# Gates of the recurrence and scores of the windowed attention as pairs of 64-row products on the two halves of the array's rows

## The chip, the core and the metric

One core of a Trainium2 chip runs the kernel in one launch. The time is the device time in microseconds of that launch; most executions of a kernel agree within 0.3%. The engines, as the profile names them: PE is TensorE's matmul, PEld its weight load, DVE is VectorE, ACT is ScalarE, POOL is GpSimd, SP issues transfers.

## What is computed

One layer of a hybrid decoder over 1024 prompt tokens and 8 sample tokens (width 1024). A combined projection feeds three branches: a convolution with a gated linear recurrence, windowed attention (window 128, 16 query heads of 64 on 4 key heads), and cross-attention into 256 memory rows. The branches are merged by gates, projected, normalised, and go through a SwiGLU block. Two places matter here.

```python
def rg_lru(xc, h0, wa, ba, wx, bx, lam):          # LRU_BLOCKS = 16, LRU_BLOCK = 64
    xblk = xf.reshape(B, T, LRU_BLOCKS, LRU_BLOCK)
    r = jax.nn.sigmoid(jnp.einsum('btni,nij->btnj', xblk, wa).reshape(B, T, C) + ba)
    i = jax.nn.sigmoid(jnp.einsum('btni,nij->btnj', xblk, wx).reshape(B, T, C) + bx)
    ...
def swa_prompt(q, k, v, sinks):                   # HEAD_DIM = 64, WINDOW = 128, blocks of 128 tokens
    s = jnp.einsum('bnqkgd,bnmkd->bnkgqm', qb, kband) * scale
    ...
    p = sink_softmax(s, mask, sinks)
```

Both contract over 64 values: a gate block has 64 inputs, a head has 64 dimensions.

## The kernel before

Everything is computed transposed: channels lie on the 128 partitions, tokens along the free dimension. Products keep almost the precision of float32 by splitting each operand into a high part `h` (float32r) and the low remainder `l`, and adding three products, h·h, h·l and l·h (`mm3`, lines 111 to 118; lines 241 to 243 are the same three in the projection). ACT writes the high part (line 77), DVE the low one (line 78).

The stages in order of time: keys and values of the memory; the projection (`project`), 30 units of seven products, each product in two halves of twelve matmuls; between its steps `pump` advances the recurrences (`lru`), one for each of the 8 slices of 128 channels, and the sample tokens' cross-attention; then the prompt's cross-attention and the windowed attention (`windows`), into which products of the branch projections (`fill`, tiles `bra` and `brc`) are laid; then the rest of the branch projections, the output projection, the SwiGLU block and the last product with its normalisation. A scheduler puts each engine's instructions into one fixed order when the kernel is built; that order is static on the chip.

**Gates** (lines 750 to 758). For each slice `m` and each third of the 1032 tokens (344 columns), the two gates are made one after the other, with a step of the projection between them. The stationary weights are 128 by 128 blocks that hold two 64 by 64 blocks on the diagonal and zeros elsewhere: `wr` is 128 by 256, one half for each gate. Each gate is three matmuls over all 128 rows into a bank of the pool tag "o" (one bank), and one tanh by ACT over 128 partitions (line 757).

**Scores** (lines 581 to 591). For each key head `kv` and block `b` of 128 queries, four heads share the keys. A head's query tile has its high part on rows 0 to 63 and its low part on rows 64 to 127; the keys' high part stands twice in `ks[0]`, their low part twice in `ks[1]`. So two matmuls over 128 rows make all four partial products: eight matmuls a block, each with 256 columns (128 in the first block of a head, b = 0, which has no predecessor). Heads 0 and 1 go to one bank of the tag "s", heads 2 and 3 to the other; two banks carry that tag, and they serve the projection's tiles `uc` as well. DVE adds the mask and takes the minimum (line 590), ACT makes the exponentials (line 594), and the transposed weights (`bt`, line 611) go into the products with the values (`bo`, lines 616 and 617).

Of the kernel before, what the change touches and what calls it, by code (L numbers as in the profile page):

```python
# [10 lines left out]
F32 = mybir.dt.float32  # L11
F32R = mybir.dt.float32r
AF = mybir.ActivationFunctionType
ALU = mybir.AluOpType
# [4 lines left out]
P = 128  # L19
D = 1024  # L20
KT = D // P
TP = 1024
# [6 lines left out]
NF = 22  # L29
# [23 lines left out]
GELU_C = math.sqrt(2.0 / math.pi)  # L53
GELU_A = math.sqrt(0.044715)

V_BG, V_CW, V_CB, V_BA, V_BX, V_LAM = 0, 24, 56, 64, 72, 80
V_G1, V_B1, V_G2, V_B2, V_SNK, V_SNKD, V_EPS, V_N = 88, 96, 104, 112, 120, 136, 137, 138


class Builder:  # L60
# [489 lines left out]
    def win_load(self, kv):  # L550

        nc, ph = self.nc, self.ph
        rows = lambda i: slice((i % 2) * 64, (i % 2) * 64 + 64)
        q = []
        ks = [ph.tile([P, TP], F32R, tag="ks", name=f"ks{kv}_{e}", bufs=4) for e in range(2)]
        for e in range(2):
            for half in range(2):
                nc.sync.dma_start(ks[e][half * 64:(half + 1) * 64].bitcast(F32), self.scr["k"][rows(kv), kv // 2, e, :])
        for g in range(4):
            st = ph.tile([P, TP], F32R, tag="st", name=f"st{kv}_{g}", bufs=6)  # L560
            for e in range(2):
                nc.sync.dma_start(st[e * 64:(e + 1) * 64].bitcast(F32), self.scr["q"][rows(g), 2 * kv + g // 2, e, :])
            q.append(st)
        vs = ph.tile([P, 8, P], F32R, tag="vs", name=f"vs{kv}", bufs=2)
        nc.sync.dma_start(vs.bitcast(F32), self.scr["v"][:, :, kv * P:(kv + 1) * P])
        return ks, q, vs

    def win_scores(self, kv, ops, b):

        nc = self.nc  # L570
        nk = 2 if b else 1
        n = nk * P
        k0 = max(b - 1, 0) * P
        msk = self.mask[:, 256 - n:]
        ks, q, _ = ops
        snk = self.nsnk[:, 4 * kv:4 * kv + 4]
        st = self.sm.tile([P, 12], F32, tag="bst", name=f"bst{kv}_{b}", bufs=4)
        p = self.ph.tile([P, 4, 257], F32, tag="p", name=f"bp{kv}_{b}", bufs=3)
        pg = [p[:, g, :n] for g in range(4)]
        nc.gpsimd.tensor_copy(p[:, :, n], snk)  # L580
        for pr in range(2):
            s = self.bank("s", f"bs{kv}_{b}_{pr}")
            for u in range(2):
                qq = q[2 * pr + u][:, b * P:(b + 1) * P]
                o = s[:, u * 256:u * 256 + n]
                nc.tensor.matmul(o, qq, ks[0][:, k0:k0 + n], start=True, stop=False)
                nc.tensor.matmul(o, qq, ks[1][:, k0:k0 + n], start=False, stop=True)
            for u in range(2):
                g = 2 * pr + u
                nc.vector.tensor_tensor_reduce(pg[g], s[:, u * 256:u * 256 + n], msk, 1.0, snk[:, g:g + 1],  # L590
                                               ALU.add, ALU.min, st[:, g:g + 1])
        for g in range(4):
            x = p[:, g, :n + 1]
            nc.scalar.activation(x, x, AF.Exp, bias=st[:, g:g + 1], scale=-1.0, accum_out=st[:, 4 + g:5 + g])  # L594
        nc.vector.reciprocal(st[:, 8:12], st[:, 4:8])
        for g in range(4):
            r = st[:, 8 + g:9 + g]
            if g % 2:
                nc.scalar.mul(pg[g], pg[g], r)
            else:  # L600
                (nc.gpsimd if g else nc.vector).tensor_scalar_mul(pg[g], pg[g], r)
        return pg
# [75 lines left out]
    def lru_consts(self):  # L678

        nc = self.nc  # L680
        lam = self.vec[:, V_LAM:V_LAM + KT]
        w = self.cst.tile([P, 8 * KT], F32, name="lruc")
        self.sp2 = w[:, 0:8]
        self.hba, self.hbx = w[:, 8:16], w[:, 16:24]
        e, z, z2, acc, t = (w[:, 24 + 8 * i:32 + 8 * i] for i in range(5))
        self.nsnk = self.cst.tile([P, 16], F32, name="nsnk")
        nc.vector.tensor_scalar_mul(self.nsnk, self.vec[:, V_SNK:V_SNK + 16], -1.0)
        self.hbg = self.cst.tile([P, 24], F32, name="hbg")
        nc.vector.tensor_scalar_mul(self.hbg, self.vec[:, V_BG:V_BG + 24], 0.5)
        nc.vector.tensor_scalar_mul(self.hba, self.vec[:, V_BA:V_BA + 8], 0.5)  # L690
        nc.vector.tensor_scalar_mul(self.hbx, self.vec[:, V_BX:V_BX + 8], 0.5)
        nc.vector.scalar_tensor_tensor(t, lam, -1.0, lam, op0=ALU.mult, op1=ALU.max)
        nc.scalar.activation(e, t, AF.Exp, scale=-1.0)
        nc.vector.tensor_scalar_add(z, e, 2.0)
        nc.vector.reciprocal(z, z)
        nc.vector.tensor_mul(z, z, e)
        nc.vector.tensor_mul(z2, z, z)
        nc.vector.memset(acc, 1.0 / 17.0)
        for d in (15, 13, 11, 9, 7, 5, 3, 1):
            nc.vector.tensor_mul(acc, acc, z2)  # L700
            nc.vector.tensor_scalar_add(acc, acc, 1.0 / d)
        nc.vector.tensor_mul(acc, acc, z)
        nc.vector.tensor_scalar(t, lam, -1.0, 0.0, op0=ALU.mult, op1=ALU.max)
        nc.vector.scalar_tensor_tensor(t, acc, 2.0, t, op0=ALU.mult, op1=ALU.add)
        nc.vector.tensor_scalar_mul(self.sp2, t, 2.0)
        self.sp4n = self.cst.tile([P, KT], F32, name="sp4n")
        nc.vector.tensor_scalar_mul(self.sp4n, t, -4.0)
# [20 lines left out]
    def lru(self, m, xr, yr):  # L728

        nc, io, vec = self.nc, self.io, self.vec  # L730
        col = lambda base: vec[:, base + m:base + m + 1]
        stt = nc.vector.scalar_tensor_tensor
        wr = self.lr.tile([P, 256], F32, tag="wlr", name=f"wlr{m}", bufs=1)
        nc.sync.dma_start(wr, io["wlru"][m])
        cw = [col(V_CW + 8 * i) for i in range(4)]
        xc = self.zt(f"xc{m}")
# [7 lines left out]
        nc.gpsimd.tensor_copy(self.pconv[:, m, :], xr[:, TP - 3:TP])  # L744
        nc.gpsimd.tensor_copy(self.scvo[:, m, 0:2, :], buf[:, 1:3, :])
        nc.gpsimd.tensor_copy(self.scvo[:, m, 2, :], xr[:, TP:T])
        wgh, wgl = (self.lr.tile([P, 256], F32R, tag=f"wg{e}", name=f"wg{e}{m}", bufs=1) for e in "hl")
        self.split(wgh, wgl, wr)
        a, ti = self.zt(f"tr{m}"), self.zt(f"ti{m}")
        for c, (t0, n) in enumerate(THIRDS):  # L750
            xch, xcl = (self.lr.tile([P, n], F32R, tag=f"xc{e}", name=f"xc{e}{m}_{c}", bufs=1) for e in "hl")
            self.split(xch, xcl, xc[:, t0:t0 + n])
            yield
            for j, (dst, hb) in enumerate(((a, self.hba), (ti, self.hbx))):
                ps = self.bank("o", f"g{m}_{j}_{c}")[:, :n]
                self.mm3(ps, [((wgh[:, j * P:(j + 1) * P], wgl[:, j * P:(j + 1) * P]), (xch, xcl))])
                nc.scalar.activation(dst[:, t0:t0 + n], ps, AF.Tanh, bias=hb[:, m:m + 1], scale=0.5)
                yield

        sp2, sp4n = self.sp2[:, m:m + 1], self.sp4n[:, m:m + 1]  # L760
# [21 lines left out]
        g = self.zt(f"ge{m}")  # L782
# [563 lines left out]
class Finish:  # L1346
# [42 lines left out]

_INS = {  # L1390
    "xT": (P, KT, T), "xQ": (2, 4, P, 4 * QN), "memT": (P, KT * NM), "wmk": (KT, P, D), "wmv": (8, P, D), "win": (60, P, D),
    "wbr": (24, P, D), "wout": (KT, P, D), "wgu": (2 * NF, P, D), "wdn": (KT, P, NF * P), "wlru": (KT, P, 256),
    "vec": (P, V_N), "cst": (P, P + 256), "scv": (P, KT, 3, NB), "sh": (P, KT, NB), "cwk": (NB, P, 256),
    "cwv": (NB, P, 256), "cwkT": (NB, P, 2, P), "cmk": (NB, NM, D), "cmvT": (NB, D, NM),
}
# [7 lines left out]
def _pack(i):  # L1403
    import numpy as np

    f = {k: np.asarray(v) for k, v in i.items()}

    def mtiles(w):
        k, m = w.shape
        return w.reshape(k // P, P, m // P, P).transpose(2, 1, 0, 3).reshape(m // P, P, k)  # L1410
# [4 lines left out]
    def cols(v):  # L1415
        return v.reshape(-1, P).T

    o = {}
    x = np.concatenate([f["x_prompt"].reshape(TP, D), f["x_sample"].reshape(NB, D)], axis=0)
# [9 lines left out]
    o["wout"] = mtiles(f["w_out"][0])  # L1429
    o["wgu"] = mtiles(f["w_gate_up"][0])  # L1430
    o["wdn"] = mtiles(f["w_down"][0])
    blk = np.zeros((KT, P, 256), np.float32)
    for j, name in enumerate(("lru_wa", "lru_wx")):
        w = f[name][0].reshape(KT, 2, 64, 64)
        for e in range(2):
            blk[:, e * 64:(e + 1) * 64, j * P + e * 64:j * P + (e + 1) * 64] = w[:, e]
    o["wlru"] = blk
    snk = f["sinks"][0]
    o["vec"] = np.concatenate(
        [cols(f["b_gates"][0]), cols(f["conv_w"][0]), cols(f["conv_b"][0]), cols(f["lru_ba"][0]), cols(f["lru_bx"][0]),  # L1440
         cols(f["lru_lambda"][0]), cols(f["ln1_g"][0]), cols(f["ln1_b"][0]), cols(f["ln2_g"][0]), cols(f["ln2_b"][0]),
         np.broadcast_to(snk, (P, 16)), np.tile(snk, NB).reshape(P, 1), np.full((P, 1), LN_EPS, np.float32)], axis=1)
    q, m = np.arange(P)[:, None], np.arange(256)[None, :]
# [47 lines left out]
```

## Time and profile before

| | us |
|---|---|
| median of 3 runs | 1975.46 |
| lowest and highest | 1969.87, 1976.79 |
| the profiled execution | 1975.36 |
| its span, first to last instruction | 1973.6 |

So 1.76 us of the profiled execution lie around its span, and it stands 0.1 us from the median. The profile is one execution on the one core. Busy shares are of the span. A matmul's duration in the trace runs from its start to the end of its results, so matmuls overlap in the trace; what a matmul costs in a row of them is the distance from its start to the next one's start, which is called its pitch below.

### The profile page before, as it was taken

How to read it: one execution, taken by the hardware profiler on the slowest of the kernel's cores; microseconds unless marked ns; L12 is line 12 of the kernel's file. 1: busy time of each engine (PE TensorE's matmuls, PEld its weight loads, DVE VectorE, ACT ScalarE, POOL GpSimd, SP SyncE). 2: the span in 40 equal slices, each digit the busy share in tenths (PEclk: the TensorE clock that was granted, in tenths of full speed). 3: DMA queues.
4: the chain of work that ended last, by engine and by line, in shares of the span. 5: the costliest groups of instructions: out<-in, count | busy, mean ns of one | idle time of the engine just before them, and what ended most of it. 6: DMA issues, size and time to landing. Idle time of an engine off the chain costs nothing.

```text
span 1973.6 us, 37334 instructions
## 1 busy us (share of the span) xinstructions
PE 1928.8 (98%) x14524; PEld 1896.1 (96%) x14524; DVE 1331.1 (67%) x2698; ACT 971.7 (49%) x2075; POOL 96.5 (5%) x152
## 2 busy tenths in 40 slices
PE   9999999999999999999999999999999999899997
PEld 9999999999999998988899999999999999899996
DVE  7878977886866664388876567775655656534267
ACT  6555565464656544397774253543343434522024
POOL 1000000010000000021220000000000000000001
PEclk9999999999999999999999999999999999899998
DMA  8554555455323367767525251222223222713112
GB/s 317 166 157 162 177 164 192 137 183 192 121 83 131 138 225 219 203 173 192 162 69 179 86 193 44 76 93 98 89 93 96 92 87 80 290 56 116 35 47 86
DMA packets 152241, 271.45 MB, mean 138 GB/s; under 512 B 18608, under 2 KB 71936, under 8 KB 152064
## 3 DMA queue, kind: packets, MB, share of 16 engines
q1 hardware_dynamic: 151296, 266.97, 41.9%
q8 instruction: 114, 1.87, 0.4%
q0 software_dynamic: 768, 2.10, 0.3%
q14 instruction: 63, 0.52, 0.1%
HBM read 200.00 MB, written 73.18 MB: 138 GB/s over the span
## 4 chain that ended last, share of the span: by engine, by line
PE 86%; DMA 5%; ACT 5%; DVE 3%; issue 1%; SPq 0%; ACTq 0%; POOL 0%; DVEq 0%; POOLq 0%
PE ub L243 5%; PE ub L241 5%; PE ub L242 5%; PE ubf L241 4%; PE ubf L242 4%; PE ubf L243 4%; PE d L116 3%; PE d L117 3%; PE d L118 3%; PE ud L243 3%; PE ud L242 3%; PE ud L241 3%; PE udf L241 2%; PE udf L242 2%; PE udf L243 2%; PE brs L116 2%
## 5 line engine op out<-in xcount | busy, mean ns | idle before, releaser
L116 PE MATMUL d<-gh,wd_h 128*128 128x384 f32 (+2 forms) x360 | 116.4, 326 | 5.2 <-ACT gh L77 5.2
L117 PE MATMUL d<-gl,wd_h 128*128 128x384 f32 (+2 forms) x360 | 116.7, 324 | 0.0
L118 PE MATMUL d<-gh,wd_l 128*128 128x384 f32 (+2 forms) x360 | 116.0, 323 | 0.0
L1216 DVE SCALAR_TENSOR_TENSOR acc<-d,acc 128x384 f32<-128x384 f32 (+2 forms) x48 | 24.6, 515 | 91.5 <-PE d L118 91.5
L116 PEld LDWEIGHTS d<-gh,wd_h 128*128 128x128 f32 x360 | 68.5, 191 | 6.3 <-ACT gh L77 5.7
L118 PE MATMUL op<-mh,wol 128*128 128x258 f32 x256 | 72.3, 282 | 1.3 <-DVE wol L78 1.3
L116 PE MATMUL op<-mh,woh 128*128 128x258 f32 x256 | 72.5, 283 | 0.0
L117 PE MATMUL op<-ml,woh 128*128 128x258 f32 x256 | 72.1, 282 | 0.0
L241 PE MATMUL ub<-th,u_4h 128*128 128x258 f32 x240 | 68.7, 286 | 3.3 <-ACT u2s L266 3.3
L594 ACT ACTIVATE bp<-bp,bst 128x257 f32<-128x257 f32 (+1 forms) x128 | 62.8, 493 | 17.3 <-DVE bst L590 17.0
L241 PE MATMUL ub<-th,u_0h 128*128 128x258 f32 x240 | 68.3, 285 | 1.4 <-ACT zb L1362 1.4
L117 PEld LDWEIGHTS d<-gl,wd_h 128*128 128x128 f32 x360 | 68.8, 191 | 0.3 <-DVE gl L78 0.3
L118 PEld LDWEIGHTS d<-gh,wd_l 128*128 128x128 f32 x360 | 68.9, 192 | 0.0
L243 PE MATMUL ub<-th,u_4l 128*128 128x258 f32 x240 | 68.8, 287 | 0.0
L242 PE MATMUL ub<-tl,u_4h 128*128 128x258 f32 x240 | 68.3, 285 | 0.0
L243 PE MATMUL uc<-th,u_3l 128*128 128x258 f32 x240 | 68.2, 284 | 0.0
L243 PE MATMUL ub<-th,u_2l 128*128 128x258 f32 x240 | 68.2, 284 | 0.0
L243 PE MATMUL ud<-th,u_5l 128*128 128x258 f32 x240 | 68.2, 284 | 0.0
L243 PE MATMUL ud<-th,u_1l 128*128 128x258 f32 x240 | 68.2, 284 | 0.0
L243 PE MATMUL ub<-th,u_0l 128*128 128x258 f32 x240 | 68.2, 284 | 0.0
L243 PE MATMUL ub<-th,u_6l 128*128 128x258 f32 x240 | 68.1, 284 | 0.0
L241 PE MATMUL ub<-th,u_6h 128*128 128x258 f32 x240 | 68.1, 284 | 0.0
(816 smaller groups left out, 7951.2 us busy)
## 6 DMA issues: line engine op xcount, KB each, us to landing
ur<-win SPq DMA_DIRECT2D x120, 256.0 KB, 3.0
urf<-wgu SPq DMA_DIRECT2D x80, 256.0 KB, 2.7
scr_f<-G SPq DMA_DIRECT2D x22, 516.0 KB, 2.8
gl<-scr_f SPq DMA_DIRECT2D x22, 516.0 KB, 8.3
dck<-cmk SPq DMA_DIRECT2D x32, 256.0 KB, 3.4
dcv<-cmvT SPq DMA_DIRECT2D x32, 256.0 KB, 3.6
st<-scr_q SPq DMA_DIRECT2D x32, 256.0 KB, 4.6
scr_g<-za SPq DMA_DIRECT2D x12, 516.0 KB, 3.4
```

Source lines behind the costliest of these rows:

```text
L116: nc.tensor.matmul(ps, sh, mh, start=opens and i == 0, stop=False)
L117: nc.tensor.matmul(ps, sh, ml, start=False, stop=False)
L118: self.last_mm = nc.tensor.matmul(ps, sl, mh, start=False, stop=closes and i == last).ins
L241: mm(sh[:, w], xh, start=opens and k == 0, stop=False)
L242: mm(sh[:, w], xl, start=False, stop=False)
L243: self.last_mm = mm(sl[:, w], xh, start=False, stop=k == 3).ins
L594: nc.scalar.activation(x, x, AF.Exp, bias=st[:, g:g + 1], scale=-1.0, accum_out=st[:, 4 + g:5 + g])
L1216: nc.vector.scalar_tensor_tensor(a, ps, 0.5, a, op0=ALU.mult, op1=ALU.add)
```

## The change

Both contractions are put on half of the array's rows each, as pairs of matmuls: one on partitions 0 to 63, one on 64 to 127, into two banks. In the gates the weights lose their zeros: the tile is 128 by 128, with the a- and x-gate blocks of the upper 64 channels side by side in rows 0 to 63 (a, x) and those of the lower 64 channels in rows 64 to 127 (x, a). A pair makes both gates of the slice: three pairs where there were two times three matmuls, and both gates come at once, into a bank "o" and a bank "s". Each bank holds 64 channels of either gate, so ACT takes four tanh of 64 partitions where it took two of 128. The biases stand in the same order.

In the scores, two heads lie on the two halves of the query tile, and high and low parts in two tiles; the partial product l·l is left out. A block takes six pairs, twelve matmuls, where it took eight. Heads 0 and 2 go to one bank, 1 and 3 to the other, and `behind` holds the twelve in this order on TensorE, without forbidding other matmuls between them. The query loads are 128 partitions high: four of 512 KB for a key head instead of eight of 256 KB.

```diff
-        for g in range(4):
-            st = ph.tile([P, TP], F32R, tag="st", name=f"st{kv}_{g}", bufs=6)
+        for i in range(2):
+            q.append([ph.tile([P, TP], F32R, tag="st", name=f"st{kv}_{i}{e}", bufs=6) for e in range(2)])
             for e in range(2):
-                nc.sync.dma_start(st[e * 64:(e + 1) * 64].bitcast(F32), self.scr["q"][rows(g), 2 * kv + g // 2, e, :])
-            q.append(st)
+                nc.sync.dma_start(q[i][e].bitcast(F32), self.scr["q"][:, 2 * kv + i, e, :])
...
+        s, last = [self.bank("s", f"bs{kv}_{b}_{r}") for r in range(2)], None
         for pr in range(2):
-            s = self.bank("s", f"bs{kv}_{b}_{pr}")
-            for u in range(2):
-                qq = q[2 * pr + u][:, b * P:(b + 1) * P]
-                o = s[:, u * 256:u * 256 + n]
-                nc.tensor.matmul(o, qq, ks[0][:, k0:k0 + n], start=True, stop=False)
-                nc.tensor.matmul(o, qq, ks[1][:, k0:k0 + n], start=False, stop=True)
-            for u in range(2):
-                g = 2 * pr + u
-                nc.vector.tensor_tensor_reduce(pg[g], s[:, u * 256:u * 256 + n], msk, 1.0, snk[:, g:g + 1],
-                                               ALU.add, ALU.min, st[:, g:g + 1])
+            o = [x[:, pr * 256:pr * 256 + n] for x in s]
+            for k, (eq, ek) in enumerate(((0, 0), (0, 1), (1, 0))):
+                for r in range(2):
+                    half = slice(64 * r, 64 * r + 64)
+                    ins = nc.tensor.matmul(o[r], q[pr][eq][half, b * P:(b + 1) * P], ks[ek][half, k0:k0 + n],
+                                           start=k == 0, stop=k == 2).ins
+                    if last:
+                        self.behind(ins, last)
+                    last = ins
+        for g in range(4):
+            o = s[g % 2][:, g // 2 * 256:g // 2 * 256 + n]
+            nc.vector.tensor_tensor_reduce(pg[g], o, msk, 1.0, snk[:, g:g + 1], ALU.add, ALU.min, st[:, g:g + 1])
...
-        wr = self.lr.tile([P, 256], F32, tag="wlr", name=f"wlr{m}", bufs=1)
+        wr = self.lr.tile([P, P], F32, tag="wlr", name=f"wlr{m}", bufs=1)
...
-            for j, (dst, hb) in enumerate(((a, self.hba), (ti, self.hbx))):
-                ps = self.bank("o", f"g{m}_{j}_{c}")[:, :n]
-                self.mm3(ps, [((wgh[:, j * P:(j + 1) * P], wgl[:, j * P:(j + 1) * P]), (xch, xcl))])
-                nc.scalar.activation(dst[:, t0:t0 + n], ps, AF.Tanh, bias=hb[:, m:m + 1], scale=0.5)
+            ps = [self.bank(tag, f"g{m}_{e}_{c}")[:, :n] for e, tag in enumerate("os")]
+            half = [slice(64 * e, 64 * e + 64) for e in range(2)]
+            for k, (w, x) in enumerate(((wgh, xch), (wgh, xcl), (wgl, xch))):
+                for e, r in enumerate(half):
+                    nc.tensor.matmul(ps[e], w[r], x[r], start=k == 0, stop=k == 2)
+            for e, r in enumerate(half):
+                for src, dst in ((half[e], a), (half[1 - e], ti)):
+                    nc.scalar.activation(dst[r, t0:t0 + n], ps[e][src], AF.Tanh,
+                                         bias=self.hbl[src, 2 * m + e:2 * m + e + 1], scale=0.5)
                 yield
```

The rest packs the gates' weights and biases in that order on the host side of the layout.

More of the change, by code (lines that the diff above doesn't have):

```diff
@@ L54 @@
 GELU_A = math.sqrt(0.044715)
-V_BG, V_CW, V_CB, V_BA, V_BX, V_LAM = 0, 24, 56, 64, 72, 80
+V_BG, V_CW, V_CB, V_BL, V_LAM = 0, 24, 56, 64, 80
 V_G1, V_B1, V_G2, V_B2, V_SNK, V_SNKD, V_EPS, V_N = 88, 96, 104, 112, 120, 136, 137, 138
@@ L683, in lru_consts @@
         self.sp2 = w[:, 0:8]
-        self.hba, self.hbx = w[:, 8:16], w[:, 16:24]
+        self.hbl = w[:, 8:24]
         e, z, z2, acc, t = (w[:, 24 + 8 * i:32 + 8 * i] for i in range(5))
@@ L689, in lru_consts @@
         nc.vector.tensor_scalar_mul(self.hbg, self.vec[:, V_BG:V_BG + 24], 0.5)
-        nc.vector.tensor_scalar_mul(self.hba, self.vec[:, V_BA:V_BA + 8], 0.5)
-        nc.vector.tensor_scalar_mul(self.hbx, self.vec[:, V_BX:V_BX + 8], 0.5)
+        nc.vector.tensor_scalar_mul(self.hbl, self.vec[:, V_BL:V_BL + 16], 0.5)
         nc.vector.scalar_tensor_tensor(t, lam, -1.0, lam, op0=ALU.mult, op1=ALU.max)
@@ L746, in lru @@
         nc.gpsimd.tensor_copy(self.scvo[:, m, 2, :], xr[:, TP:T])
-        wgh, wgl = (self.lr.tile([P, 256], F32R, tag=f"wg{e}", name=f"wg{e}{m}", bufs=1) for e in "hl")
+        wgh, wgl = (self.lr.tile([P, P], F32R, tag=f"wg{e}", name=f"wg{e}{m}", bufs=1) for e in "hl")
         self.split(wgh, wgl, wr)
@@ L1391 @@
     "xT": (P, KT, T), "xQ": (2, 4, P, 4 * QN), "memT": (P, KT * NM), "wmk": (KT, P, D), "wmv": (8, P, D), "win": (60, P, D),
-    "wbr": (24, P, D), "wout": (KT, P, D), "wgu": (2 * NF, P, D), "wdn": (KT, P, NF * P), "wlru": (KT, P, 256),
+    "wbr": (24, P, D), "wout": (KT, P, D), "wgu": (2 * NF, P, D), "wdn": (KT, P, NF * P), "wlru": (KT, P, P),
     "vec": (P, V_N), "cst": (P, P + 256), "scv": (P, KT, 3, NB), "sh": (P, KT, NB), "cwk": (NB, P, 256),
@@ L1431, in _pack @@
     o["wdn"] = mtiles(f["w_down"][0])
[L1432 to L1437, printed above, removed]
+    wa, wx = (f[n][0].reshape(KT, 2, 64, 64) for n in ("lru_wa", "lru_wx"))
+    o["wlru"] = np.stack([np.concatenate([wa[:, 0], wx[:, 0]], axis=2), np.concatenate([wx[:, 1], wa[:, 1]], axis=2)],
+                         axis=1).reshape(KT, P, P)
+    ba, bx = (f[n][0].reshape(KT, 2, 64) for n in ("lru_ba", "lru_bx"))
+    bl = np.stack([np.concatenate([ba[:, 0], bx[:, 0]], axis=1), np.concatenate([bx[:, 1], ba[:, 1]], axis=1)], axis=1)
     snk = f["sinks"][0]
     o["vec"] = np.concatenate(
-        [cols(f["b_gates"][0]), cols(f["conv_w"][0]), cols(f["conv_b"][0]), cols(f["lru_ba"][0]), cols(f["lru_bx"][0]),
+        [cols(f["b_gates"][0]), cols(f["conv_w"][0]), cols(f["conv_b"][0]), cols(bl),
          cols(f["lru_lambda"][0]), cols(f["ln1_g"][0]), cols(f["ln1_b"][0]), cols(f["ln2_g"][0]), cols(f["ln2_b"][0]),
```

## The prediction

> **What bounds the kernel now.** I began with the page: busy shares, then the chain that ended last.
>
> ```profile
> span 1973.6 us, 37334 instructions
> ...
> PE 1928.8 (98%) x14524; PEld 1896.1 (96%) x14524; DVE 1331.1 (67%) x2698; ACT 971.7 (49%) x2075; POOL 96.5 (5%) x152
> ...
> PE 86%; DMA 5%; ACT 5%; DVE 3%; issue 1%; SPq 0%; ACTq 0%; POOL 0%; DVEq 0%; POOLq 0%
> ```
>
> TensorE is busy from end to end and carries 86% of the chain; its weight loads are as many as its matmuls (14524 each). Then the stretches of the two stages that change, the projection while it makes gates (114 to 640) and the windows (831 to 1045). The columns are the stretch, its length, and busy us with counts of PE, PEld, DVE, ACT and POOL, then the granted clock, the DMA share and GB/s.
>
> ```profile
> 114.00:640.00 526.00, 522.25 (x4291) 520.42 (x4290) 410.87 (x829) 301.93 (x572) 29.48 (x35) 1.00 0.47 155
> 831.00:1045.00 214.00, 207.35 (x1333) 191.42 (x1333) 174.38 (x538) 162.40 (x488) 41.51 (x61) 1.00 0.55 150
> ```
>
> At full clock TensorE lacks 4 us of 526 in the first and 7 of 214 in the second. What leaves its stream shortens the run, nearly all in the first stage, less surely in the second.
>
> What a matmul costs is its pitch, not its duration. In the timeline (start, duration, engine, line, names) a gate in its surroundings reads:
>
> ```profile
> 113.97 0.33 PE L116 MATMUL g<-xch,wgh 128*128 128x344 f32 x1
> 113.97 0.19 PEld L117 LDWEIGHTS g<-xcl,wgh 128*128 128x128 f32 x1
> ...
> 114.13 0.32 PE L117 MATMUL g<-xcl,wgh 128*128 128x344 f32 x1
> 114.13 0.19 PEld L118 LDWEIGHTS g<-xch,wgl 128*128 128x128 f32 x1
> ...
> 114.29 0.32 PE L118 MATMUL g<-xch,wgl 128*128 128x344 f32 x1
> ...
> 114.44 0.28 PE L241 MATMUL ub<-th,u_4h 128*128 128x258 f32 x1
> ```
>
> Three matmuls in 114.44 - 113.97 = 0.47 us: 0.157 each for 344 columns. The next weights begin to load as a matmul starts. The scores, in the same view:
>
> ```profile
> 846.52 0.28 PE L586 MATMUL bs<-ks,st 128*128 128x256 f32 x1
> 846.64 0.28 PE L587 MATMUL bs<-ks,st 128*128 128x256 f32 x1
> 846.76 0.28 PE L586 MATMUL bs<-ks,st 128*128 128x256 f32 x1
> 846.88 0.28 PE L587 MATMUL bs<-ks,st 128*128 128x256 f32 x1
> 847.00 0.34 PE L118 MATMUL bra<-baH,wba_l 128*128 128x384 f32 x1
> ```
>
> Four in 0.48 us: 0.12 each for 256 columns. And a second limit close under it, from the chain (eight transposes of 128 columns) and the timeline (eight products of only 8 columns, up to the start of the next matmul):
>
> ```profile
> 789.89 0.87 PE cpt L514 x8
> ...
> 737.92 0.96 PE L884 MATMUL dss<-dqb,dsk 128*128 128x8 f32 x8
> 738.74 0.36 PE L116 MATMUL cs<-mkh,cqh 128*128 128x256 f32 x1
> ```
>
> 0.87/8 = 0.109 and 0.82/8 = 0.103: with 128 columns to stream or with 8, the pitch hardly differs. What they share is a load of 128 columns of weights each. I take 0.109 us as the floor that one weight load sets; at 256 columns a product stands just above it.
>
> **The change part by part.** How often, from the listings by line:
>
> ```profile
> L116 PE MATMUL g<-xch,wgh x48: 322/326/326, 114.0 to 635.7; 128*128 128x344 f32 x48
> ...
> L586 PE MATMUL bs<-ks,st x128: 220/283/366, 831.7 to 1030.6; 128*128 128x256 f32 x112, 128*128 128x128 f32 x16
> ...
> L757 ACT ACTIVATE ti<-g,lruc x24: 527/548/557, 118.0 to 636.5; 128x344 f32<-128x344 f32 x24
> ```
>
> *Gates.* 48 gates of three matmuls are 24 groups of six, 144 matmuls: 144 x 0.157 = 22.6 us. After: 24 groups of three pairs. If the two of a pair stream at once, a pair costs one pitch: 72 x 0.157 = 11.3. Saved 11.3 us. In the built order all 24 groups are unbroken, so every matmul has its partner beside it.
>
> *Scores.* Twice the listing's counts (L587 has the same): 224 of 256 columns and 32 of 128, 224 x 0.12 + 32 x 0.109 = 30.4 us. After: 336 and 48, of half height. But here the built order does not keep the pairs together: the scheduler puts matmuls of the branches, transposes and value products between them, and the 32 blocks come out as 98 fragments, 19 of them a single matmul, 28 a single pair. A fragment of odd length leaves one matmul without partner. Rounding each up to pairs, I count 189 pitches of 256 columns and 29 of 128: 189 x 0.12 + 29 x 0.109 = 25.8. Saved 4.6 us, where whole pairs would save 7.6 (192 pitches).
>
> *Going over between whole and half height.* 24 + 98 = 122 fragments, so 244 crossings. No row has a product of 64 rows. The nearest change of shape is a transpose that uses 8 columns of the array, between two products of 128:
>
> ```profile
> 81.88 0.28 PE L243 MATMUL ub<-th,u_6l 128*128 128x258 f32 x1
> 81.99 0.38 PE L800 MATMUL drt_c<-ident,qdc 128*8 128x128 f32 x2
> 82.13 0.37 PE L241 MATMUL ub<-th,u_0h 128*128 128x258 f32 x1
> 82.33 0.28 PE L242 MATMUL ub<-tl,u_0h 128*128 128x258 f32 x1
> ```
>
> From 81.88 to 82.33 are 0.45 us; two products at 0.12 and two transposes at 0.109 make 0.458. So there both crossings together cost nothing. That is the lower end, 0. The upper end is that the array must be empty first: a matmul's results end 0.28 after its start and the next could have started at 0.12, so 0.16 us. I take 0.025, near the row that I have, but not on it, since that row narrows the columns and here the rows are cut: 244 x 0.025 = 6.1 us. The Trainium skill, in TensorEngine Tiling (Array Packing), Key Properties, says that changing the tiling mode drains TensorE; by it the crossings would stand at the upper end. The trace of before disagrees with it for narrow columns and cannot say for rows.
>
> *ACT.* Four tanh of 64 partitions stand for two of 128. Half the partitions do not halve the time: two copies of 256 columns, of 8 and of 64 partitions, read
>
> ```profile
> L801 ACT COPY drow_c<-drt_c x4: 343/351/361, 82.9 to 393.0; 8x256 f32<-8x256 f32 x4
> ...
> L621 ACT COPY bob<-bo x64: 353/368/372, 848.1 to 1045.0; 64x256 f32<-64x256 f32 x64
> ```
>
> So ACT gets 48 more of 0.548, 26.3 us, in a stage where it is busy 302 of 526. Its idle time covers that. What it can delay are the banks: a gate now also holds a bank "s", which the next `uc` needs, and behind its four tanh stand the copies of the weights. Uncovered, 24 x 2 x 0.548 = 26 us; the nearest rows are the waits on ACT that TensorE has there today:
>
> ```profile
> PEld ub L241 <- ACT zb L1362: 2.0, 3, 1.1
> ...
> DVE bp L590 <- PE bs L587: 2.9, 5, 0.9
> ...
> PEld bo L616 <- ACT bph L77: 9.2, 26, 1.7
> ```
>
> (total us, times, longest). I take as much again, 2 us, with 0 and 6 as ends, since weights are copied three steps ahead. The two rows of the windows say that DVE waits for the scores 2.9 us in all, while TensorE already waits 9.2 us for ACT's copies. DVE can start a block only after ten or eleven products rather than two, and a block needs both banks at once; branch products fill both gaps, so nothing for it, and its failure would be in the same ends.
>
> *The rest.* Sixteen query loads of 512 KB for 32 of 256 KB, half the gate weights to load and split, one constant operation fewer: all beside TensorE's stream, nothing.
>
> *Sum.* -11.3 - 4.6 + 6.1 + 2.0 = -7.8 us. The profiled execution took 1975.36 (span 1973.6 and 1.76 around it), the median of the runs is 1975.46; so **1967.6 us**. With the ends of crossings (0 to 0.05, twice my value, within this case) and waits (0 to 6): -15.9 to +2.3, 1959.5 to 1977.7.
>
> **Rivals.**
>
> *The weight loads of a pair do not run side by side.* Each half-height matmul still loads 128 columns of weights. If these loads go one after the other, every one of the 528 costs 0.109, whatever streams: gates 144 x 0.109 = 15.7 (-6.9), scores 384 x 0.109 = 41.9 (+11.5). With 2 us of waits and crossings from 0 to 6.1: 1982.0 to 1988; I take the lower, as a crossing hides behind a load that is late anyway. For it: in every row above a load starts only when the matmul before it has started. Against it: those are all on the same rows. The Trainium skill, TensorE: Matmul & The Clock Gate, Part 3, The mechanism, has loads for another row group pulled ahead of running matmuls and tiles about 4 ns apart; that favours my forecast, and no run here shows it yet.
>
> *The array empties at each crossing.* This is the slower side. 244 x 0.16 = 39.0 in place of 6.1: -15.9 + 39.0 + 2 = +25.1, **2000.5 us**. The gain is eaten where a crossing costs more than 13.9/244 = 0.057 us, and it is over 0.5% slower above 0.098. The fragments decide: 196 of the 244 crossings are in the windows, for 4.6 us of saving. For it: nothing in the trace crosses between row heights, so nothing excludes it. Against: the 8-column rows.
>
> *The two of a pair run one after the other*, so that the change does not do what it says. Gates unchanged, scores 336 x 0.12 + 48 x 0.109 = 45.6, +15.2; with 2 us of waits 1992.5. Nothing in the profile speaks for it but that no pair has been seen.
>
> **How the numbers follow.** Pairs run at once with cheap crossings: 0.45. Weight loads in turn: 0.25. Emptying: 0.18. No concurrency: 0.12. About 0.5% (9.9 us) is what a measurement of this kernel tells from no change; its three runs lie 6.9 apart. Faster by that means under 1965.6, a crossing under 0.016: half of the first case, 0.23. Slower means over 1985.3: all of the last two, and a fifth of the second, 0.35. The rest, 0.42, is the same. The range reaches from the lower end of the first case to the emptying array, 1959 to 2001, and leaves out the upper half of that one and what lies beyond the ends. The likeliest case's own range is 1959.5 to 1977.7.
>
> **What would show it.** Right: in a gate's timeline two matmuls start within hundredths of a us, pairs 0.157 apart, six in 0.47, and the step before and after as today. Rival one: starts 0.109 apart, six in 0.65. No concurrency: six in 0.94. Emptying: a hole of 0.16 before the first half-height and the next full-height matmul, in the windows some 98 times each way. The stretch 114 to 640 should be 9 to 11 us shorter by the matmuls alone; the windows about the same. I am wrong if the windows lose more than 10 us, if `uc` waits for ACT, or if the pairs' pitch is over 0.2.

## The result and the profile after

The changed kernel takes 2008.28 us (median of 4 runs, 2004.84 to 2010.31), the kernel before 1972.66 on the same chip: a ratio of 1.017 with a 95% interval of [1.0152, 1.0187], or +30 to +37 us. Intervals in brackets below are of the same kind. It is slower, and beyond the upper end of my range (2001). The profiled execution took 2008.17 us.

The page of the kernel after, its span, engines and chain:

```profile
span 2006.4 us, 37590 instructions
...
PE 1955.7 (97%) x14652; PEld 1887.3 (94%) x14652; DVE 1333.1 (66%) x2697; ACT 999.8 (50%) x2123; POOL 99.1 (5%) x152
...
PE 81%; DMA 7%; DVE 6%; ACT 4%; issue 1%; SPq 0%; ACTq 0%; DVEq 0%; POOL 0%; POOLq 0%
```

TensorE's share of the chain fell from 86 to 81%, although it has 128 matmuls more. By the pitches its work fell by the 15.9 us that were forecast; what grew are holes. (Its busy time is 27 us longer all the same, since a matmul that waits for its weights is recorded as longer: 0.42 us against 0.33 in the rows below.) A gate's timeline, matmuls first, weight loads second (start, duration, engine, line, names; x2 is a pair):

```profile
137.92 0.28 PE L243 MATMUL ub<-th,u_2l 128*128 128x258 f32 x1
138.13 0.42 PE L759 MATMUL g<-xch,wgh 64*128 64x344 f32 x2
138.39 0.33 PE L759 MATMUL g<-xcl,wgh 64*128 64x344 f32 x2
138.55 0.32 PE L759 MATMUL g<-xch,wgl 64*128 64x344 f32 x2
138.80 0.39 PE L241 MATMUL uc<-th,u_3h 128*128 128x258 f32 x1
139.02 0.29 PE L242 MATMUL uc<-tl,u_3h 128*128 128x258 f32 x1
```

```profile
138.12 0.19 PEld L759 LDWEIGHTS g<-xch,wgh 64*128 64x128 f32 x2
138.23 0.19 PEld L759 LDWEIGHTS g<-xcl,wgh 64*128 64x128 f32 x2
138.39 0.19 PEld L759 LDWEIGHTS g<-xch,wgl 64*128 64x128 f32 x2
138.80 0.19 PEld L241 LDWEIGHTS uc<-th,u_3h 128*128 128x128 f32 x1 [0.22 <-issue]
138.91 0.19 PEld L242 LDWEIGHTS uc<-tl,u_3h 128*128 128x128 f32 x1
```

Three readings. First, the pairs work: the two matmuls of a pair start 3 to 5 ns apart in the trace, two loads of 0.18 us both end within 0.19, and the third pair follows the second at 0.16. Second, before the first pair TensorE does not load the pair's weights while the product before is running, as it does between products of one height. The product starts at 137.92, its 258 columns take 0.12, the load starts only at 138.12. The pair streams from 138.23; I read this from the next load, which begins as a matmul starts. 0.19 us are lost. Third, the same on the way out: 138.55 + 0.157 = 138.71, the first product of `uc` streams from 138.91: 0.20 lost. Each crossing is thus about 0.09 in which nothing loads or streams, which I read as the array emptying (the profile does not name it), and 0.106 for a weight load that nothing covers. From 137.92 to 139.02 are 1.10 us, the pitches make 0.12 + 3 x 0.157 + 0.12 = 0.71. Over the 24 fragments of the gates the median of this excess is 0.399 us; 21 of them lie between 0.397 and 0.400, and the other three (0.6 to 3.1) hold a wait as well.

In the windows the fragments are short and the crossings many; here one matmul alone:

```profile
861.46 0.28 PE L117 MATMUL bra<-baL,wba_h 128*128 128x258 f32 x1
861.67 0.38 PE L586 MATMUL bs<-ks,st 64*128 64x256 f32 x1
861.98 0.39 PE L118 MATMUL bra<-baH,wba_l 128*128 128x258 f32 x1
862.21 0.28 PE L116 MATMUL bra<-baH,wba_h 128*128 128x258 f32 x1
```

From 861.46 to 862.21 are 0.75 us for three products of 0.12. The view of the tile `bs` names the idle time of the engines before the scores and before DVE's reading of them. In the kernel before it has no row for TensorE there; now it begins (us in all, times)

```profile
  issue: 18.4, 71
  PE bs L586: 18.1, 16
```

The first row is TensorE: 18.4 us in 71 times, in which it waited for nothing that the profile shows. The second is DVE waiting for the scores; it was 2.9 us in 5 times before.

### The profile page after: what moved, and what is told of

The parts are those of the page before. It is cut to its first block, busy times and chain, and to the rows that moved or that the text cites. A ratio compares the mean times of both kernels' runs of the same rounds, so it can differ in the third digit from the quotient of the medians.

```text
span 2006.4 us, 37590 instructions
## 1 busy us (share of the span) xinstructions
PE 1955.7 (97%) x14652; PEld 1887.3 (94%) x14652; DVE 1333.1 (66%) x2697; ACT 999.8 (50%) x2123; POOL 99.1 (5%) x152
## 4 chain that ended last, share of the span: by engine, by line
PE 81%; DMA 7%; DVE 6%; ACT 4%; issue 1%; SPq 0%; ACTq 0%; DVEq 0%; POOL 0%; POOLq 0%
PE ub L241 4%; PE ub L242 4%; PE ub L243 4%; PE ubf L241 4%; PE ubf L242 4%; PE ubf L243 4%; PE d L116 3%; PE d L117 3%; PE d L118 3%; PE ud L241 2%; PE ud L243 2%; PE ud L242 2%; PE udf L241 2%; PE udf L242 2%; PE udf L243 2%; PE bs L586 2%
## 5 line engine op out<-in xcount | busy, mean ns | idle before, releaser
L241 PE MATMUL uc<-th,u_3h 128*128 128x258 f32 x240 | 68.4, 285 | 1.2 <-ACT ti L762 1.2
L241 PE MATMUL ud<-th,u_5h 128*128 128x258 f32 x240 | 68.4, 285 | 0.0
L241 PE MATMUL ud<-th,u_1h 128*128 128x258 f32 x240 | 68.2, 284 | 0.0
```

What stands on the lines that cost most here:

```text
L241: mm(sh[:, w], xh, start=opens and k == 0, stop=False)
```

## The experiments

The theory after this reading (A): pairs stream side by side, but each of the 244 crossings costs 0.195 us. Rivals: ACT's doubled tanh and the second bank (B), and scores that wait for two banks at once (C).

**The gates alone.** The part of the diff in `lru` with its weights and biases; `win_load` and `win_scores` as before.

> Only the gates are changed; the scores are as before. Theory A (pairs stream side by side, but every crossing between whole and half height empties the array and leaves one weight load uncovered, 0.195 us each as the profile after shows it): 24 unbroken groups, 48 crossings, -11.3 + 48 x 0.195 = -1.9 us, with up to 2 us of waits: -2 to 0 us against the kernel before. Theory B (the loss comes from the four tanh and the second bank that a gate holds, so from ACT): most of the loss is here, +10 us or more, with waits of TensorE for ACT between 114 and 640 us.

Measured: 1980.01 us, ratio 1.0037 [1.0024, 1.005], +5 to +10 us. A alone is refuted here: it gave -2 to 0. The 24 fragments cost 0.399 each as it said, so some 9 us (7.3 less -1.7) come from elsewhere.

**The scores alone.** The rest of the diff.

> Only the scores are changed; the gates are as before. Theory A: 98 fragments, 196 crossings, -4.6 + 196 x 0.195 = +33.6 us. Theory B (ACT and banks of the gates): +5 us or less. Theory C (the scores wait for DVE, since a block now needs both banks of its tag at once): about +33 us too, but as waits of TensorE for DVE and not as holes at every change of height.

Measured: 2000.16 us, ratio 1.0137 [1.0124, 1.015], +24 to +30. Most of the loss is here, somewhat less than A's +33.6. Between the last product of the projection and the first of the output projection, the traces give 445.3 us before and 469.6 here. The pitches of the products are 414.5 and 410.0; 98 fragments at 0.399 are 39.1; what is left is 30.9 before and 20.5 here. The stage is not the same in every execution: in the ten profiles here whose windows have the old code it takes 440.4 to 445.6 us, which leaves 25.9 to 31.1. So, if a fragment costs here what it costs in the gates, 5 to 11 us of the holes lie over waits that TensorE had in this stage anyway. This is a remainder and was not measured by itself.

**The scores alone, a block's products together** (the diff is against the run before this one).

```diff
+            with self.tc.high_priority():
                 for k, (eq, ek) in enumerate(((0, 0), (0, 1), (1, 0))):
...
+                        elif self.last_read:
+                            self.tc.add_manual_dep(ins, self.last_read.name, mybir.DependencyInfo(
+                                mybir.DependencyClass.Sync, mybir.DependencyReason.DATA), reason="both banks")
```

> As the run with the scores alone changed, but a block's twelve half-height matmuls stay together: they have a high priority, and the first one waits until DVE has read both banks of the block before. The same products in 35 fragments instead of 98, 70 crossings instead of 196. Theory A: -7.6 + 70 x 0.195 = +6 us. Theory C (waits for both banks): the wait for both banks stands at the head of every block, so the loss stays at +25 to +34 us.

Measured: 1981.46 us, ratio 1.0041 [1.0026, 1.0055], +5 to +11: A's +6, and not C's +25 to +34. The trace has the 35 fragments that were expected. The timeline of a block:

```profile
901.07 0.28 PE L118 MATMUL bra<-baH,wba_l 128*128 128x258 f32 x1
901.28 0.97 PE L587 MATMUL bs<-ks,st 64*128 64x256 f32 x12
902.18 0.39 PE L116 MATMUL bra<-baH,wba_h 128*128 128x258 f32 x1
902.41 0.28 PE L117 MATMUL bra<-baL,wba_h 128*128 128x258 f32 x1
```

1.34 us against 0.12 + 6 x 0.12 + 0.12 = 0.96: again 0.38 too much, but once for six pairs. The same 384 products with 126 fewer crossings are 19 us faster than in the run before. A would give 25 for the crossings and 3 for whole pairs; the difference fits holes that lay over waits there. Even unbroken they lose: a block saves two pitches, 0.24 us, and pays 0.4.

**The gates without half height, by stacking.**

```diff
+            for e, x in enumerate(xs):
+                src = xc[half[e], t0:t0 + n]
+                nc.scalar.copy(x[half[e]], src)
+                nc.vector.tensor_sub(x[half[1 - e]], src, x[half[e]].bitcast(F32))
...
+                for k, w in enumerate((wgh, wgl)):
+                    nc.tensor.matmul(ps, w[:, e * P:(e + 1) * P], x, start=k == 0, stop=k == 1)
```

> The gates in another way, without half height: the high part of a block of 64 channels lies on one half of the rows and its remainder on the other, and the block's weights for both gates stand twice, so that two whole-height matmuls make both gates of a block (four for a slice and third instead of six; the product of the two remainders is included). The scores are as before. TensorE loses 48 matmuls of 0.157 us and crosses nothing. ACT gets four tanh of 64 partitions instead of two of 128 and one more cast, DVE one more subtraction, for each slice and third: some 37 us for ACT. Theory A: -7.5 us, with waits -7.5 to -4. Theory B (ACT's extra work is what costs): no gain, up to +10 us.

Measured: 1972.78 us, ratio 0.9997 [0.9985, 1.0009]. No gain that can be told (-3.0 to +1.8 us), though TensorE has 48 matmuls less, 7.5 us. Between 60 and 700 us its weight loads wait 13.7 us in all where they waited 8.5 before, so waits took back some 5 us of it. Who causes them is not shown. The tile `xc` shows DVE behind ACT's casts, 19.7 us in 21 waits:

```profile
  ACT xc L754: 19.7, 21
```

**The gates of the change at whole height.**

```diff
-                    nc.tensor.matmul(ps[e], w[r], x[r], start=k == 0, stop=k == 2)
+                    nc.tensor.matmul(ps[e], w[:, e * P:(e + 1) * P], x, start=k == 0, stop=k == 2)
```

> Gates of the change with whole-height products: the same six matmuls in one group, the same two banks, the same four tanh of 64 partitions, but the weights are 128 by 128 blocks with zeros for the other half's rows, so nothing pairs and nothing crosses. Scores as before. It holds all of the change of the gates but the height. Crossings alone (theory A): 0 us against the kernel before, while gates alone stood at +7. Waits for banks, DVE and ACT (theory B, now as a second cause beside the crossings): the waits that the run with gates alone showed stay, +7 to +9 us.

Measured: 1981.62 us, ratio 1.0036 [1.0025, 1.0048], +5 to +9.5. Without a crossing or a pair it loses the same as the gates of the change. So the height of the gates cannot be told from nothing here, as -11.3 + 9.6 = -1.7 would have it (either interval is 5 us wide), and the +7 are the rest of the edit. Among its waits of the weight loads between 115 and 640 us (total us, times, longest) are

```profile
PEld g L757 <- DVE za L268: 4.4, 2, 2.6
...
PEld uc L241 <- ACT ti L760: 1.6, 3, 0.6
```

Neither stood there before: a gate waits for DVE to read `uc`, whose bank it now needs, and `uc` waits for ACT to read the gate. All waits of the weight loads between 60 and 700 us add up to 15.8 us, against 8.5 in the kernel before: +7.3, for +7.1 measured.

**A crossing by itself.** Three kernels, each the kernel before with 100 small matmuls of one kind (`w` and `x` are the weights and the input of the product behind each):

```diff
                 d = self.bank("t", f"ud{u}_{p}")
...
+                nc.tensor.matmul(d[:, 400:408], w[:, :P], x[:, 0, :8], start=True, stop=True)     # whole
+                nc.tensor.matmul(d[:, 400:408], w[:64, :P], x[:64, 0, :8], start=True, stop=True) # half height
+                nc.tensor.matmul(d[:64, 400:408], w[:, :64], x[:, 0, :8], start=True, stop=True)  # half width
```

> The kernel before with 100 added matmuls of 8 columns, whole height and whole width, each between two products of the projection and of the SwiGLU block, into unused columns of a bank that is about to be opened; their results are not used. The yardstick for the next two: 100 x 0.109 = +11 us by every theory.

> The same 100 added matmuls of 8 columns on rows 0 to 63 alone, with no pairs, no second bank and no change in the other engines' work: 200 crossings. Theory A: 11 + 200 x 0.2 = +51 us. If the holes in the changed kernel come from pairs, banks or waits and not from the height: +11 us.

> The same 100 added matmuls of 8 columns, whole height but on 64 columns of the array: 200 changes of width. If every change of shape empties the array: +51 us as with half height. If only the height does, as the 8-column transposes of the kernel before suggest: +5 to +11 us (half the weights to load).

Measured: 1984.5, 2011.31 and 1984.61 us; ratios to before 1.0045 [1.0023, 1.0067], 1.0185 [1.016, 1.021] and 1.0053 [1.0034, 1.0072]. Whole height costs +9 us (11 expected), half width the same within the noise, half height 27 us more (its two runs lie 0.3 apart). The same place in each timeline, whole height, half height, half width:

```profile
499.35 0.32 PE L118 MATMUL g<-xch,wgl 128*128 128x344 f32 x1
499.50 0.17 PE L261 MATMUL ud<-th,u_1h 128*128 128x8 f32 x1
499.53 0.37 PE L241 MATMUL ud<-th,u_1h 128*128 128x258 f32 x1
499.73 0.28 PE L242 MATMUL ud<-tl,u_1h 128*128 128x258 f32 x1
```

```profile
506.16 0.32 PE L118 MATMUL g<-xch,wgl 128*128 128x344 f32 x1
506.41 0.27 PE L261 MATMUL ud<-th,u_1h 64*128 64x8 f32 x1
506.61 0.39 PE L241 MATMUL ud<-th,u_1h 128*128 128x258 f32 x1
506.84 0.28 PE L242 MATMUL ud<-tl,u_1h 128*128 128x258 f32 x1
```

```profile
496.63 0.32 PE L118 MATMUL g<-xch,wgl 128*128 128x344 f32 x1
496.78 0.17 PE L261 MATMUL ud<-th,u_1h 128*64 128x8 f32 x1
496.81 0.37 PE L241 MATMUL ud<-th,u_1h 128*128 128x258 f32 x1
497.01 0.29 PE L242 MATMUL ud<-tl,u_1h 128*128 128x258 f32 x1
```

0.38, 0.68 and 0.38 us from first to last. Over all 100 places the medians are 0.352, 0.633 and 0.350, so half height adds 0.28 us, 28 in all, for 27 measured. My +40 between them (51 against 11) was a slip: the small product's load of 0.109 is already one of the two uncovered loads, so it must not be added to them. No pair, second bank or work of another engine differs between the three, so the hole belongs to the height. Using 64 columns in place of 128 leaves no such hole.

**What else the gates paid for.** Both gates at once in two banks, with two tanh as before; and apart from it the tanh as twice 64 partitions.

```diff
+            ps = [self.bank(tag, f"g{m}_{j}_{c}")[:, :n] for j, tag in enumerate("os")]
...
+                for r in (slice(0, 64), slice(64, 128)):
+                    nc.scalar.activation(dst[r, t0:t0 + n], ps[r], AF.Tanh, bias=hb[r, m:m + 1], scale=0.5)
```

> The kernel before with one thing of the change alone: both gates of a slice and third are made at once, in a bank of the tag o and one of the tag s, with no step of the projection between them. Whole height, two tanh of 128 partitions as before. It splits the +7 us of the run with gates of whole height. If the bank that is shared with the projection's tiles and the lost step between the gates cost it (theory D): +5 to +7 us. If the doubled tanh do (theory E): 0 to +2 us.

> The kernel before with the other half: each tanh of 128 partitions is made as two of 64, everything else as before, so ACT has 48 more instructions of 0.548 us, 26 us, in the projection. Theory D (bank and order): 0 to +2 us. Theory E (ACT's time): +5 to +7 us.

Measured: 1976.8 us, 1.0016 [1.0005, 1.0028], and 1973.83 us, 1.0002 [0.9992, 1.0012]. The second bank and the lost step cost +1.0 to +5.5 us, where D gave +5 to +7; ACT's 26 us alone cost -1.6 to +2.4, so E falls. The middles, 3.2 and 0.4, make half of the +7.1 of both together. That four tanh also hold the shared bank longer would explain the rest. The traces point that way: the row of `uc` waiting for ACT, 1.6 us above, stands in neither of these two, and the waits of the weight loads between 60 and 700 us are 4.0 and 0.5 above those of the kernel before, where both together have 7.3. But the intervals overlap and no run has this alone; it stays open.

**Stacked gates with the casts on GpSimd**: `nc.gpsimd.tensor_copy` for `nc.scalar.copy`.

> The stacked gates (four whole-height matmuls for a slice and third instead of six, nothing crosses), with the casts of the high parts on GpSimd instead of ACT, since the stacked gates gained nothing (ratio 0.9997) although TensorE had 48 matmuls less. If ACT's 37 us ate the 7.5 us, ACT now has 23 us less than there: -3 to -6 us. If it was DVE that stood in its queue behind the casts (20 us of waits there): GpSimd is slower, DVE waits longer, 0 to +10 us.

Measured: 1973.98 us, 1.0001 [0.9992, 1.0009]. No gain again, so the -3 to -6 of one theory did not come. DVE did not wait longer either, as the other had it: its waits behind the casts fell from 19.7 to 7.3 us. So these waits alone do not explain the missing gain. The weight loads still wait 13.2 us between 60 and 700, and what causes it stays open. None of the versions tried beats the kernel before.

## Why the prediction was wrong

*What bounds, and the pitches*: right. TensorE's stream sets the time, and the pitches of 0.157 and 0.12 came back in the pairs.

*Pairs at once*: right, and so the rivals of weight loads in turn and of no concurrency fall. The Trainium skill's Part 3 of TensorE: Matmul & The Clock Gate (The mechanism), with loads for another row group pulled ahead and tiles about 4 ns apart, agrees with the 3 ns here.

*The count of fragments*: right, 122 in the built order and in the trace.

*Crossings*: the step that failed. I took 0.025 us from the 8-column transposes, where fewer columns of the array are used, and carried it over to rows. The half-width run shows that these rows were true of width, and the half-height run that they said nothing of height: 0.2 us each. The upper end, 0.16, was wrong too. It counted the time until a product's results are out, where the traces show the next load after 0.09, and it left out that nothing covers this load, 0.106 more. That put the emptying rival, which was the right mechanism, at 2000.5 instead of beyond. 244 x 0.2 = 48.8 stands where the sum had 6.1. With 0.2 the rival's own sum would be +34.9, near the +33.5 measured, but by luck: its 2 us for the banks were too few, it had no holes over waits, and the two errors nearly cancel. The Trainium skill's rule in TensorEngine Tiling (Array Packing), Key Properties, that changing the tiling mode drains TensorE, agrees with the hole at a change of height. For width there is no such hole (0.350 against 0.352 us); but the traces give the rows and columns in use and not the tiling mode, so whether the rule fails there, as my prediction had it for the transposes, no run shows.

*ACT and banks*: 2 us with 6 as the end were too few. In the gates the rest of the edit costs 7.1 (run at whole height). I had one direction of the shared bank, `uc` waiting for ACT, and its size was about right (1.6 us in that run). I did not have the other, the gate waiting for DVE to read `uc` (4.4), because I sized the term by waits of a kernel in which the two did not share.

*Windows*: "about the same" was wrong by the crossings, 27 us for the scores alone; 5 to 11 us of theirs seem to lie over waits, which I had not counted. That DVE waits longer for the scores, which I took as nothing, did come, 18.1 us for 2.9. It did not reach TensorE as far as the waits show: its weight loads wait 8.5 us for ACT's copies where they waited 9.2.

The sum with these terms: -15.9 + 48.8 + 7.1, less 5 to 11, is +29 to +35, for +33.5 measured [30.0, 36.9]; gates alone and scores alone add to +34.

## What to carry to other kernels

Half-height products run in pairs for the price of one, but a fragment of them between whole-height products costs 0.4 us before it saves anything, at the 344 and 256 columns here three or four pairs' worth; count the fragments in the built order, not the products in the source. A price measured for one change of shape does not hold for another: ask what the rows at hand have in common with the new case. And a bank borrowed from a busy tag is a cost of its own, which shows when the rest of the edit is run without its point.

## What the runs showed of the hardware

Going between matmuls of 128 and of 64 rows keeps the next weights from loading while the last product runs: about 0.09 us until the load starts, which I read as the array emptying, and 0.106 for the load, each way; that is 0.28 us more for one small product in a stream (0.633 against 0.352). Going between 128 and 64 columns costs nothing that can be seen (0.350). Two half-height weight loads of 0.18 us run side by side, and the two matmuls of a pair start 3 to 5 ns apart.
